# A later transposition, later weight sums and other buffer counts in a two-layer trunk kernel

## The chip, the cores and the metric

The kernel runs on one core of a Trainium2 chip. The metric is the device time in microseconds of one execution: 992.76 us is the median of 3 runs (991.8 to 993.68).

## The reference

The reference is a decoder trunk of two layers on 256 tokens of width 1024. Each layer is a half-step SwiGLU FFN, a token-mixing sublayer with one input projection and one output projection, and a second FFN, each followed by a layer norm:

```python
def swiglu(x, w_gate, w_up, w_down):
    return (jax.nn.silu(x @ w_gate) * (x @ w_up)) @ w_down

for l in range(DEPTH):
    x = layer_norm(ALPHA * x + 0.5 * swiglu(x, ffn1_gate[l], ffn1_up[l], ffn1_down[l]), ...)
    ...                                  # mixing: short conv, spatial gating, sparse attention
    x = layer_norm(ALPHA * x + mix, ...)
    x = layer_norm(ALPHA * x + 0.5 * swiglu(x, ffn2_gate[l], ffn2_up[l], ffn2_down[l]), ...)
```

All weights are float32, and the inner width of an FFN is 2816. The change touches the FFNs alone, and the pools from which all stages take their buffers.

## The kernel before

**Split weights.** Every product is made of three matmuls, of a rounded high part and a remainder of each operand (`mm3`, L246, and L258 to L260). A block of the weight stream (128x1024, 512 KB) is loaded into a `raw` buffer by SyncE; ScalarE casts it to a `hi` tile (L190), and VectorE subtracts to get the `lo` tile (L191). There are 5 `raw`, 12 `hi` and 12 `lo` buffers. A `hi` or `lo` buffer comes free when the last matmul that reads it has ended; `raw` when VectorE has read it. `ensure` (L167) writes the blocks down in the order of the stream, some seven blocks ahead of the product that needs them.

**Order.** The program is written in the order of the code. A planner with a cost model of its own then lays out each engine's queue before the run: it goes through simulated time and gives a free engine the earliest written instruction that is ready and for which a buffer is free (silu and product in the chunks of 256 count as written somewhat earlier, L544, L560). On the chip each queue runs in the order so fixed, and an instruction that waits holds up those behind it.

**FFN.** The inner width is cut into a chunk 0 of 512 columns and nine chunks of 256. In chunk 0 the products keep tokens on the partitions: gate of tile 0 (`pg`), up of tile 0 (`pu`), gate of tile 1, up of tile 1 (`tok`, L398), each 24 matmuls of 512 columns. Their PSUM banks alternate between two (`gu_bank`, L149), so that up of tile 1 is written to the bank of up of tile 0, and gate of tile 1 to that of gate of tile 0. ScalarE makes `sg` (silu, L421), VectorE `h = pu * sg` (L426, called `product`). `h` is transposed by TensorE (`trans`, L435, four transpositions of 128x128), copied to `hf` (L443) and split into `hTh` and `hTl` (L263). In the chunks of 256 the products have the inner width on the partitions (`chan`, L408, 48 matmuls of 256 columns) and need no transposition.

**Paired chunks.** In three of the four FFNs (all but the first of layer 0) the down products of chunks 0 to 5 are made with seven matmul triples M1 to M7 in place of eight (`paired`, L476). Their right operands come from two `raw` blocks of the stream (`pair_operands`, L196): M1 from a tile `b11` (one tile holds both its parts), M2 and M3 from the halves of the second block, M4 to M7 from sums of quarters of both. The sums are subtractions of 128x512 in place in `raw` (L202); the casts of the two summed blocks to four tiles stand in `rest` (L219), which is put off until at least two more blocks of the stream are loaded, counted whenever a block is split (L193). M5 and M7 read the first, M4 and M6 the second of these. The left operands of M1, M2, M4 are parts of `hT`; those of M3, M5, M6, M7 come from `left_sums` (L458), four small VectorE sums `S` and one split into `hTh` and `hTl`. While chunks are paired, gate and up of a chunk share one PSUM bank, so up waits until `sg` has been read from it. Between gate and up of chunk c stand M1, M2, M4, M5 of chunk c-1 (12 matmuls of 512 columns, in chunk 0 twice as many); behind up stand M6, M7, M3. M3 has a bank of its own, which a later chunk uses. `combine` (L487) adds the seven results to the residual.

Of the kernel before, what the change touches and what calls it, by code (L numbers as in the profile page):

```python
# [34 lines left out]
def _paired(l, f):  # L35

    return 0 if (l, f) == (0, 1) else 6
# [95 lines left out]
def _build(tc, A, out):  # L133
# [3 lines left out]
    with ExitStack() as es:  # L137
        pool = lambda name, bufs, **k: es.enter_context(tc.tile_pool(name=name, bufs=bufs, **k))
        cst = pool("cst", 1)
        rawp = pool("raw", 5)  # L140
        hip = pool("hi", 12)
        lop = pool("lo", 12)
        wk = pool("wk", 9)
        sm = pool("sm", 3)
        lnp = pool("lnp", 1)
# [3 lines left out]
        def gu_bank(shape, name):  # L149
            turns.append(1)  # L150
            return ps.tile(shape, F32, name=name, tag=f"gu{len(turns) % 2}", bufs=1)
# [9 lines left out]
        loaded = []  # L161
# [3 lines left out]
        put_off = []  # L165

        def ensure(i):  # L167
            while len(loaded) <= min(i, len(plan) - 1):
                key, k, n, split, o = plan[len(loaded)]
                src = A["ws"][o:o + 128 * n].rearrange("(p c) -> p c", p=128)  # L170
                if len(key) == 4 and key[2] == "d" and key[3] < _paired(*key[:2]):
                    raw = rawp.tile([128, n], F32, name="raw", tag="raw")
                    stream.append(SP.dma_start(raw, src))
                    if k % 2 == 0:
                        loaded.append(raw)
                    else:
                        loaded[-1], rest = pair_operands(loaded[-1], raw)
                        loaded.append(loaded[-1])
                        put_off.append((len(loaded), rest))
                    continue  # L180
                if not split:
                    raw = (hip, lop)[k % 2].tile([128, n], F32, name="w1", tag=("hi", "lo")[k % 2])
                    SP.dma_start(raw, src)
                    loaded.append((raw, None))
                    continue
                raw = rawp.tile([128, n], F32, name="raw", tag="raw")
                stream.append(SP.dma_start(raw, src))
                hi = hip.tile([128, n], F32R, name="hi", tag="hi")
                lo = lop.tile([128, n], F32R, name="lo", tag="lo")
                splits.append((ACT.copy(hi, raw),  # L190
                               DVE.tensor_tensor(lo, raw, hi.bitcast(F32), ALU.subtract)))  # L191
                loaded.append((hi, lo))
                while put_off and put_off[0][0] < len(loaded) - 1:  # L193
                    put_off.pop(0)[1]()

        def pair_operands(ra, rb):  # L196
# [39 lines left out]
        def kslices(key, n, ahead=None):  # L236

            res = []
            for hi, lo in blocks(key, ahead):
                m = hi.shape[1] // n  # L240
                res += [(hi[:, i * n:(i + 1) * n], lo[:, i * n:(i + 1) * n]) for i in range(m)]
            return res
# [3 lines left out]
        def mm3(o, a, b, start, stop):  # L246

            PE.matmul(o, lhsT=a[0], rhs=b[0], start=start, stop=False)  # L248
            PE.matmul(o, lhsT=a[0], rhs=b[1], start=False, stop=False)  # L249
            return PE.matmul(o, lhsT=a[1], rhs=b[0], start=False, stop=stop)  # L250
# [34 lines left out]
        def xT(t, k):  # L285
            c = slice(t * 128, t * 128 + 128)
            return xTh[:, k, c], xTl[:, k, c]
# [102 lines left out]
        def ffn(l, f, lni, last=False, mid=None):  # L390
            n = len(CHUNKS)
            paired_chunks = _paired(l, f)
# [5 lines left out]
            def tok(name, t, in_y=False, ahead=None):  # L398

                w = kslices((l, f, name, 0), 512, ahead)  # L400
                if in_y:
                    p = ps.tile([128, 512], F32, name="p" + name, tag="y", bufs=4)
                else:
                    p = gu_bank([128, 512], "p" + name)
                products[:] = [mm3(p, xT(t, k), w[k], k == 0, k == KC - 1) for k in range(KC)]
                return p
# [17 lines left out]
            def product(p, sg):  # L424
                h = wk.tile([128, 512], F32, name="h", tag="w")
                DVE.tensor_tensor(h, p.rearrange("p a b -> p (a b)") if len(p.shape) == 3 else p, sg, ALU.mult)  # L426
                return h
# [3 lines left out]
            def hpair():  # L431
                return (wk.tile([128, 512], F32R, name="hTh", tag="a"),
                        wk.tile([128, 512], F32R, name="hTl", tag="a"))

            def trans(h, t):  # L435
                tr = ps.tile([128, 512], F32, name="tr", tag="tr")
                for i in range(4):
                    c = slice(i * 128, i * 128 + 128)
                    PE.transpose(tr[:, c], h[:, c], ident)
                hT[0, t] = hpair()  # L440
                if paired_chunks:
                    hf[t] = wk.tile([128, 4, 128], F32, name="hf", tag="w")
                    ACT.copy(hf[t].rearrange("p a b -> p (a b)"), tr)  # L443
                    tr = hf[t].rearrange("p a b -> p (a b)")
                split_to(*hT[0, t], tr)
# [30 lines left out]
            def paired(c, ms):  # L476

                for m in ms:
                    if m not in M:
                        tag, bufs = {3: (held, 1), 6: ("tr", 2), 7: ("tr", 2)}.get(m, ("y", 4))  # L480
                        M[m] = ps.tile([128, 512], F32, name=f"M{m}", tag=tag, bufs=bufs)
                    for i in range(CHUNKS[c][1] // 256):
                        w = blocks((l, f, "d", c))[2 * i]
                        mm3(M[m], left_side(c, i, m), w[m], c == 0 and i == 0,
                            c == paired_chunks - 1 and i == CHUNKS[c][1] // 256 - 1)
# [36 lines left out]
            h = {}  # L522
            if l == 0 and f == 1:
                sg = [gated(tok("g", 0, True, ahead=0))]
                with ExitStack() as order:
                    for i in second_x(products):
                        order.enter_context(tc.issue_after(i.ins))
                    ensure(index[l, f, "g", 0][-1] + 3)
                sg.append(gated(tok("g", 1, True)))
                h = {t: product(tok("u", t), sg[t]) for t in range(2)}  # L530
                trans(h[0], 0)
            else:
                for t in range(2):
                    sg = gated(tok("g", t))
                    if t == 1:
                        trans(h[0], 0)
                    h[t] = product(tok("u", t), sg)

            if paired_chunks:
                turns.append(1)  # L540
                free, held = f"gu{len(turns) % 2}", f"gu{1 - len(turns) % 2}"
            for c in range(1, n):
                p = chan("g", c)
                with tc.high_priority(offset=60):  # L544
                    sg = gated(p)
                if c == 1:
                    trans(h[1], 1)
                if c <= paired_chunks:
                    if c == 1:
                        for i in range(2):  # L550
                            a = lambda t, b: hf[t][:, 2 * i + b, :]
                            left_sums(0, i, a(0, 0), a(0, 1), a(1, 0), a(1, 1))
                    paired(c - 1, (1, 2, 4, 5))
                elif not paired_chunks:
                    if c > 1 and c - 2 < n - late:
                        down([c - 2], 1)
                    if c - 1 < n - late:
                        down([c - 1], 0)
                pu = chan("u", c)
                with tc.high_priority(offset=60):  # L560
                    hc = product(pu, sg)
                if c <= paired_chunks:
                    paired(c - 1, (6, 7, 3))
                hT[c] = hpair()
                split_to(*hT[c], hc)
                if c < paired_chunks:
                    a = lambda t, b: hc[:, b * 256 + t * 128:b * 256 + t * 128 + 128]
                    left_sums(c, 0, a(0, 0), a(0, 1), a(1, 0), a(1, 1))
                if c == paired_chunks:
                    combine()  # L570
                if c == 2:
                    with tc.issue_after(stream[-1].ins):
                        gb = load_ln(l, lni)
                if c == 4 and mid:
                    with tc.issue_after(stream[-1].ins):
                        mid()
# [362 lines left out]
```

## Time and profile before

| | |
|---|---|
| median of 3 runs | 992.76 us (991.8 to 993.68) |
| the profiled execution | 994.34 us, of which the span from first to last instruction is 992.6 us |
| TensorE (PE) busy | 969.1 us, 98% of the span |
| TensorE weight load (PEld) | 875.8 us, 88% |
| VectorE (DVE) | 734.8 us, 74% |
| ScalarE (ACT) | 512.3 us, 52% |
| mean granted TensorE clock | 0.999 |
| weight blocks (512 KB), issue to landing | 4.6 us median |

Times in the rows are microseconds from the first instruction unless marked ns. In a timeline a row is: start, length, engine, line of the kernel, operation, what it writes and reads, shape, count, and in brackets how long the engine had been idle before it and what ended that. `x4` means four instructions merged in one row. PE overlaps matmuls, so a row's length is more than the step from one start to the next.

### The profile page before, as it was taken

The numbers are of one execution on the slowest core, as the hardware profiler recorded it, in microseconds if no ns is written. First come the engines' busy times: TensorE is split into PE (matmuls) and PEld (weight loads), VectorE is DVE, ScalarE is ACT, GpSimd is POOL, SyncE is SP. The second block draws the span as 40 slices with busy tenths as digits, with TensorE's granted clock in tenths as the row PEclk, the third lists the DMA queues.
The fourth block names the chain that finished last, engine by engine and source line by source line (L and its number), as shares of the span: only waits on it lengthen the run. The fifth ranks groups of instructions, "written<-read, shape, count | busy, mean of one in ns | idle before, by whom it ended". The sixth has DMA issues, their size and how long they took to land.

```text
span 992.6 us, 16879 instructions
## 1 busy us (share of the span) xinstructions
PE 969.1 (98%) x6765; PEld 875.8 (88%) x6765; DVE 734.8 (74%) x1094; ACT 512.3 (52%) x730; POOL 19.8 (2%) x42
## 2 busy tenths in 40 slices
PE   7999999999999999999999999999999999999996
PEld 5899999899878799999879899998988778989995
DVE  5755454586869978877598888848678797888844
ACT  6644444256556655555255556534475555556520
POOL 1000000010000000000000000000000000000000
PEclk9999999999999999999999999999999999999999
DMA  7977566284323557677245667764742245757611
GB/s 256 344 237 226 181 194 193 96 324 147 111 86 128 179 180 236 194 253 233 86 151 171 233 214 253 237 200 148 256 149 80 84 158 170 253 196 232 213 60 43
DMA packets 53069, 183.19 MB, mean 185 GB/s; under 512 B 6656, under 2 KB 7168, under 8 KB 52992
## 3 DMA queue, kind: packets, MB, share of 16 engines
q1 hardware_dynamic: 52992, 182.12, 55.0%
q8 instruction: 53, 0.87, 0.4%
q14 instruction: 24, 0.20, 0.1%
HBM read 181.05 MB, written 1.05 MB: 183 GB/s over the span
## 4 chain that ended last, share of the span: by engine, by line
PE 74%; DVE 11%; DMA 9%; issue 3%; ACT 3%; SPq 0%; DVEq 0%; ACTq 0%
DMA raw<-in_ws 8%; PE pu L258 6%; PE pu L260 6%; PE pu L259 6%; PE pg L258 5%; PE pg L260 5%; PE pg L259 5%; PE y L248 4%; PE y L250 4%; PE y L249 4%; DVE raw L202 3%; PE pc L258 3%; PE pc L260 3%; PE pc L259 3%; DVE lo L263 3%
## 5 line engine op out<-in xcount | busy, mean ns | idle before, releaser
L191 DVE TENSOR_TENSOR lo<-raw,hi 128x1024 fp32r<-128x1024 f32 (+3 forms) x284 | 336.6, 1200 | 115.2 <-ACT hi L190 113.5
L190 ACT CAST hi<-raw 128x1024 fp32r<-128x1024 f32 (+3 forms) x284 | 289.8, 1034 | 247.4 <-PE pu L259 64.7
L258 PE MATMUL pu<-xTh,hi 128*128 128x256 f32 x576 | 161.7, 281 | 3.4 <-ACT sg L421 3.4
L258 PE MATMUL pg<-xTh,hi 128*128 128x256 f32 x576 | 161.6, 281 | 0.5 <-DVE h L426 0.5
L260 PE MATMUL pu<-xTh,lo 128*128 128x256 f32 x576 | 160.9, 279 | 0.0
L260 PE MATMUL pg<-xTh,lo 128*128 128x256 f32 x576 | 160.8, 279 | 0.0
L259 PE MATMUL pu<-xTl,hi 128*128 128x256 f32 x576 | 160.8, 279 | 0.0
L259 PE MATMUL pg<-xTl,hi 128*128 128x256 f32 x576 | 160.8, 279 | 0.0
L258 PEld LDWEIGHTS pu<-xTh,hi 128*128 128x128 f32 x576 | 108.0, 188 | 7.1 <-ACT sg L421 5.9
L263 ACT CAST hi<-raw 128x1024 fp32r<-128x1024 f32 x63 | 66.2, 1052 | 90.5 <-DVE raw L202 46.5
L258 PEld LDWEIGHTS pg<-xTh,hi 128*128 128x128 f32 x576 | 108.1, 188 | 2.3 <-DVE h L426 1.2
L259 PEld LDWEIGHTS pu<-xTl,hi 128*128 128x128 f32 x576 | 107.9, 187 | 1.2
L260 PEld LDWEIGHTS pu<-xTh,lo 128*128 128x128 f32 x576 | 108.2, 188 | 0.2
L259 PEld LDWEIGHTS pg<-xTl,hi 128*128 128x128 f32 x576 | 107.9, 187 | 0.5
L260 PEld LDWEIGHTS pg<-xTh,lo 128*128 128x128 f32 x576 | 108.2, 188 | 0.0
L263 DVE TENSOR_TENSOR lo<-raw,hi 128x1024 fp32r<-128x1024 f32 x63 | 76.7, 1219 | 30.6 <-ACT hi L263 21.7
L258 PE MATMUL pc<-xTh,hi 128*128 128x256 f32 x256 | 73.0, 285 | 0.5 <-DVE kd L630 0.5
L248 PE MATMUL y<-hi,hTh 128*128 128x512 f32 x184 | 72.4, 394 | 0.0
L260 PE MATMUL pc<-xTh,lo 128*128 128x256 f32 x256 | 72.4, 283 | 0.0
L259 PE MATMUL pc<-xTl,hi 128*128 128x256 f32 x256 | 71.8, 281 | 0.0
L250 PE MATMUL y<-hi,hTl 128*128 128x512 f32 x184 | 71.8, 390 | 0.0
L249 PE MATMUL y<-lo,hTh 128*128 128x512 f32 x184 | 71.6, 389 | 0.0
(188 smaller groups left out, 1702.0 us busy)
## 6 DMA issues: line engine op xcount, KB each, us to landing
raw<-in_ws SPq DMA_DIRECT2D x312, 512.0 KB, 4.6
w<-in_ws SPq DMA_DIRECT2D x8, 512.0 KB, 6.2
lng<-in_ln SPq DMA_DIRECT2D x6, 512.0 KB, 6.8
lnb<-in_ln SPq DMA_DIRECT2D x6, 512.0 KB, 7.7
raw<-in_ws SPq DMA_DIRECT2D x8, 256.0 KB, 4.8
raw<-in_ws SPq DMA_DIRECT2D x4, 420.0 KB, 4.3
x<-in_x SPq DMA_DIRECT2D x4, 256.0 KB, 5.6
out<-x SPq DMA_DIRECT2D x4, 256.0 KB, 2.1
```

The lines of the kernel that those rows point to most:

```text
L190: splits.append((ACT.copy(hi, raw), DVE.tensor_tensor(lo, raw, hi.bitcast(F32), ALU.subtract)))
L191: DVE.tensor_tensor(lo, raw, hi.bitcast(F32), ALU.subtract)))
L202: sub = lambda o, i, j: DVE.tensor_tensor(o, i, j, ALU.subtract)
L248: PE.matmul(o, lhsT=a[0], rhs=b[0], start=start, stop=False)
L249: PE.matmul(o, lhsT=a[0], rhs=b[1], start=False, stop=False)
L250: return PE.matmul(o, lhsT=a[1], rhs=b[0], start=False, stop=stop)
L258: PE.matmul(p[:, b, :], lhsT=hi, rhs=xTh[:, k, :], start=k == 0, stop=False)
L259: PE.matmul(p[:, b, :], lhsT=hi, rhs=xTl[:, k, :], start=False, stop=False)
L260: PE.matmul(p[:, b, :], lhsT=lo, rhs=xTh[:, k, :], start=False, stop=k == KC - 1)
L263: return ACT.copy(hi, src), DVE.tensor_tensor(lo, src, hi.bitcast(F32), ALU.subtract)
```

## The change

It moves the transposition of `h` of tile 0 behind up of tile 1 in the FFNs with paired chunks; it asks for three more blocks, in place of two, before `rest` is written down (for the first pair of an FFN the count is passed at the same block either way, since the second pair counts too); it exchanges the places of M3 and M4; and it takes 7 `raw` buffers and 11 `hi` and 11 `lo`, so that the memory taken stays the same.

```diff
-        rawp = pool("raw", 5)
-        hip = pool("hi", 12)
-        lop = pool("lo", 12)
+        rawp = pool("raw", 7)
+        hip = pool("hi", 11)
+        lop = pool("lo", 11)
...
-                while put_off and put_off[0][0] < len(loaded) - 1:
+                while put_off and put_off[0][0] < len(loaded) - 2:
                     put_off.pop(0)[1]()
...
                 for t in range(2):
                     sg = gated(tok("g", t))
-                    if t == 1:
+                    if t == 1 and not paired_chunks:
                         trans(h[0], 0)
                     h[t] = product(tok("u", t), sg)
+                if paired_chunks:
+                    trans(h[0], 0)
...
-                    paired(c - 1, (1, 2, 4, 5))
+                    paired(c - 1, (1, 2, 3, 5))
...
-                    paired(c - 1, (6, 7, 3))
+                    paired(c - 1, (6, 7, 4))
```

All FFNs that take the branch with the moved `trans` have paired chunks.

## Rows read from the trace of the kernel before

**Rows 1.** The page: busy time, share of the span, instructions of each engine.

```profile
PE   969.1 (98%) x6765; PEld 875.8 (88%) x6765; DVE 734.8 (74%) x1094; ACT 512.3 (52%) x730; POOL 19.8 (2%) x42
```

**Rows 2.** Waits of PE: who waited for whom, us in total, times, longest.

```profile
PE tr L439 <- DVE h L426: 4.5, 3, 1.8
PE pu L258 <- ACT sg L421: 3.4, 6, 1.2
PE pg L258 <- DVE h L426: 0.5, 1, 0.5
```

**Rows 3.** Timeline of PE, second FFN of layer 0, end of gate of tile 1.

```profile
329.34 0.39 PE L249 MATMUL pg<-lo,xTh 128*128 128x512 f32 x1
329.57 0.40 PE L250 MATMUL pg<-hi,xTl 128*128 128x512 f32 x1
331.74 0.63 PE L439 MATMUL tr<-ident,h 128*128 128x128 f32 x4 [1.77 <-DVE h L426]
332.12 0.48 PE L248 MATMUL pu<-hi,xTh 128*128 128x512 f32 x1
```

**Rows 4.** Timeline of PE at the same place of the second FFN of layer 1.

```profile
818.65 0.63 PE L439 MATMUL tr<-ident,h 128*128 128x128 f32 x4 [1.50 <-DVE h L426]
```

**Rows 5.** Timeline of DVE before the first of these stalls.

```profile
324.49 1.28 DVE L202 TENSOR_TENSOR raw<-raw 128x512 f32<-128x512 f32 x2
325.69 1.22 DVE L191 TENSOR_TENSOR lo<-raw,hi 128x1024 fp32r<-128x1024 f32 x1
...
329.17 1.22 DVE L263 TENSOR_TENSOR lo<-raw,hi 128x1024 fp32r<-128x1024 f32 x1
...
330.91 0.68 DVE L426 TENSOR_TENSOR h<-pu,sg 128x512 f32<-128x512 f32 x1
```

**Rows 6.** Timeline of ACT in the same stretch: casts of weight blocks.

```profile
319.80 1.04 ACT L190 CAST hi<-raw 128x1024 fp32r<-128x1024 f32 x1
...
325.81 1.06 ACT L263 CAST hi<-raw 128x1024 fp32r<-128x1024 f32 x1 [4.00 <-DVE raw L202]
327.20 1.05 ACT L263 CAST hi<-raw 128x1024 fp32r<-128x1024 f32 x1 [0.34 <-PE pg L250]
```

**Rows 7.** Timeline of ACT before two silus in paired chunks.

```profile
383.13 1.05 ACT L263 CAST hi<-raw 128x1024 fp32r<-128x1024 f32 x1 [2.05 <-DVE raw L202]
384.09 0.58 ACT L421 ACTIVATE sg<-pg 128x512 f32<-128x512 f32 x1
...
432.25 1.05 ACT L190 CAST hi<-raw 128x1024 fp32r<-128x1024 f32 x1 [1.60 <-DMA raw<-in_ws]
```

**Rows 8.** Timeline of PE in paired chunks, six places.

```profile
384.73 0.38 PE L258 MATMUL pu<-xTh,hi 128*128 128x256 f32 x1 [0.52 <-ACT sg L421]
...
400.28 0.39 PE L248 MATMUL M<-hi,hTh 128*128 128x512 f32 x1
...
524.99 0.28 PE L258 MATMUL pg<-xTh,hi 128*128 128x256 f32 x1
...
853.61 0.39 PE L248 MATMUL M<-hi,hTh 128*128 128x512 f32 x1
...
869.76 0.39 PE L248 MATMUL M<-hi,hTh 128*128 128x512 f32 x1
...
872.00 0.38 PE L258 MATMUL pu<-xTh,hi 128*128 128x256 f32 x1 [0.72 <-ACT sg L421]
```

**Rows 9.** Timeline of DVE at three of these places.

```profile
518.16 1.23 DVE L191 TENSOR_TENSOR lo<-raw,hi 128x1024 fp32r<-128x1024 f32 x1 [0.80 <-ACT hi L190]
...
849.94 0.69 DVE L263 TENSOR_TENSOR hTl<-S,hTh 128x512 fp32r<-128x512 f32 x1
...
869.03 0.69 DVE L263 TENSOR_TENSOR hTl<-S,hTh 128x512 fp32r<-128x512 f32 x1
```

**Rows 10.** Waits of ACT for a freed buffer of gate weights.

```profile
ACT hi L190 <- PE pg L259: 45.4, 37, 2.9
```

**Rows 11.** Busy time of each engine in the first 40 us of one FFN.

```profile
312.00:352.00 40.00, 38.23 (x205) 32.10 (x204) 36.78 (x54) 23.27 (x29) 0.99 (x1) 1.00 0.53 175
```

## The prediction, made before the changed kernel was run

> **What bounds the kernel now.** I read the page first, then the waits of TensorE, then the timelines around each of them. The page shows PE busy for 969.1 of 992.6 us [rows 1]: matmuls follow one another, 0.23 us apart at 512 columns (329.57 − 329.34, [rows 3]). DVE is second with 74%. So the order of the work matters only where PE stands still, or where it would begin to. The waits of PE that lie in the FFNs are three [rows 2]: 4.5 us in 3 waits for `h` (the transposition of tile 0, once in each FFN with paired chunks), 3.4 us in 6 waits of `pu` for `sg`, and 0.5 us for a product. Together 8.4 us, 0.85% of the span; that is the most that these edits can win. No row of PE's waits names a split weight, so the weights are always early.
>
> **Part 1: `trans` of tile 0 behind up of tile 1.** Gate of tile 1 ends its starts at 329.57, the transposition starts at 331.74 after 1.77 us of idling, and up of tile 1 comes right behind it at 332.12 [rows 3]; in layer 1's second FFN the idle time is 1.50 us [rows 4], and the three are the 4.5 us [rows 2]. It looks as if PE waited for something that it could do later. But up of tile 1 goes to the PSUM bank of up of tile 0, and that bank is free only when `h` of tile 0 has been read from it. Moved to the front, `pu` waits for the same instruction at 330.91 to 331.59 [rows 5]. By itself this edit wins nothing and costs nothing: the four transpositions are as many as before, and behind up of tile 1 they find `h` ready for 5 us. What follows from them (copy, split, left sums) is late by about one product, 24 × 0.23 = 5.5 us, but M1 needs it only after gate of chunk 1, 48 matmuls later, and the left sums wait for tile 1 anyway.
>
> The Trainium skill (PSUM — Partial Sum Buffer, "PSUM bank collisions raise a hardware error") says that two engines must be kept apart by the bank, whatever addresses in it they touch. By that rule the stall outlives the moved transposition, and the sum would lack its first term; the rows agree as far as they go, since `pu` never starts before `h` ends.
>
> What decides is therefore when DVE does `h` of tile 0. Gate of tile 1 began at 329.57 − 23 × 0.23 = 324.3, so up of tile 0 had ended by 324.5; yet `h` starts at 330.91: DVE works without a break through weight sums (L202) and casts [rows 5], and over these 40 us it is busy for 36.78 [rows 11]. Its queue is laid out by the planner: whatever is written earlier and ready goes first. Three remainders of 1.22 us stand before `h`: of a gate block of chunk 1 (325.69) and of the first pair's two summed blocks (the second at 329.17). Why were they ready? Count the `hi` buffers when gate of tile 1 starts: four for gate, four for up, 1 for one `b11` (the other is in `lo`), 2 for the second blocks of the pairs: 11. The twelfth holds the gate block of chunk 1, cast at 319.80 [rows 6], before any gate block of chunk 0 is free. The next casts, 325.81 and 327.20, take buffers that gate of tile 1 gives back, the second explicitly (`PE pg`).
>
> **Part 2: 11 `hi` and `lo`.** With 11 buffers that block can't be cast at 319.80. It waits for the first gate block to come free, at about 325.7, and its remainder is ready at 326.8 rather than in time for 325.69. The summed blocks follow one buffer later each, 1.4 us (6 × 0.23) apart. From 324.5 on the planner then finds DVE between the links of the chain of weight sums with no cast ready, and `h`, ready since 324.5, is next. I expect it at 325 to 328, before gate of tile 1 ends at 330. Then PE doesn't stop: −4.5 us in three places. The other end: the planner keeps the order. The third gate block is free at 324.3 + 3 × 1.4 = 328.5, cast by 329.5, its remainder done by 330.7, and with one sum of 0.68 us behind it `h` starts at 331.4, 0.5 us later than now: +1.5 in three places. I take −4.5, because the row at 319.80 shows that it was the twelfth buffer which let the cast in.
>
> The price of a buffer less elsewhere is lead. A paired chunk takes 7.5 buffers of each kind (2 gate, 2 up, 3.5 for the pair) in about 16 us, so one is 2.1 us. The least lead of a split weight over its first matmul in the FFNs after the first is the second gate block of chunk 1 in the FFN of layer 1: remainder done at 518.16 + 1.23 = 519.39 [rows 9], first used at 524.99 [rows 8], 5.6 us. 2.1 leaves 3.5 us: nothing. If the lead were used up by two buffers more, each late buffer would show as up to 2.1 us at PE. M3 ahead of M5 also gives the second block's tiles back in the first group, some 9 us earlier, which pays for part of the twelfth buffer.
>
> The Trainium skill (Perfetto Trace Analysis, "Optimization Strategy") reads a gap that repeats as a sign that there are too few buffers for the next tile. By that rule 11 would lengthen the three stalls: the +1.5 end, 6 us above my sum. Here the rows speak against it: the gap ends with `h`, not with a cast, and what stands in the way is work let in early.
>
> **Part 3: weight sums cast a block later, 7 `raw`.** `sg` at 384.09 stands behind a cast that waited 2.05 us for a weight sum of DVE [rows 7], and `pu` idles 0.52 us for it [rows 8]. Of the six waits for `sg` four are of this kind (2.65 us, the first 0.52 and the last 0.72 [rows 8]); in the other two (0.70 us) the cast ahead of `sg` waited for a DMA, as the one at 432.25 did for 1.60 us. With `rest` a block later an up block, whose data need no sum, is in that place, and with 7 `raw` it has been loaded sooner (a pair holds its two `raw` buffers a block longer, so of two added one is left). Bounds: all 3.9 us of `sg` and `pg` gone; or the up block waits there for a buffer, 45.4/37 = 1.23 us in the mean [rows 10], at four places: 4.9 − 2.65 = +2.3. I take half of the 2.65: −1.3. The sums' own users lose nothing: the block cast at 383.13 is read by M5 at 400.28 [rows 7, 8]. More DMAs in flight (two blocks) cost nothing, since PE waits for none behind the first.
>
> **Part 4: M4 behind M3.** M3 starts where M4 did and so needs the left sums 3 × 0.23 = 0.7 us sooner than M5 does now. In the 15 chunks 1 to 5 of three FFNs the margin from the remainder of `S` to that place runs from 0.05 us (869.71 to 869.76) to 2.98 us (850.63 to 853.61) [rows 8, 9]; the remainder is read only by the third matmul, 0.46 us on. As it stands no M3 waits. If `S` comes one cast (1.22 us) later, four chunks wait, 1.4 us in all. I take +0.3. In chunk 0 both M3 and M5 wait for `S`, and up of chunk 1, 5.7 us, is there to be put between. M4's later end holds a pair of `hT` buffers longer; 8 of the 9 are then taken, none is missing.
>
> **Sum.** −4.5 − 1.3 + 0.3 = −5.5 us: a span of 987.1 and, with the 1.7 us around it, 988.8 for the profiled execution (994.3). That execution is 1.6 us over the median, so the median comes to 992.8 − 5.5 = **987.3 us**.
>
> **Rivals.** *The stall stays.* `h` remains where it is in DVE's queue and `pu` waits in place of the transposition. Only parts 3 and 4 count: 992.8 − 1.0 = 991.8. For it: DVE is 92% busy there, and the sums' chain alone is written before `h`. Against: the casts that filled the gaps lack a buffer.
>
> *M3 waits for the left sums.* The three FFNs keep DVE so busy that `S` ends two casts (2.44 us) later than now, since up blocks and sums have traded places. Then 11 of the 15 chunks wait, 9.05 us by their margins, and even with the 4.5 us won the time is 992.8 + 9.05 − 4.5 = 997.3. It decides from a delay of about 1.9 us. Behind a waiting M3 stand M5 and up of the next chunk, so PE stops. For it: the margin of 0.05 us. Against: in the chunks shown the summed blocks' casts come behind `S`, so a later cast does not push it.
>
> *Everything goes.* All 8.4 us: 984.4. The edits do aim at each wait, but a queue fixed by a model rarely meets all.
>
> **Chances.** Forecast 0.55, stall stays 0.22, M3 waits 0.15, everything 0.08. A measurement of this kernel tells 0.2% (2 us) from no change: below 990.8 is faster, above 994.7 slower. Faster: 0.52 of the forecast, 0.02 of the second (its part 3 can win more), 0.08: 0.62. Same: 0.03 + 0.14 = 0.17. Slower: 0.06 (the second with +1.5 and +2.3) + 0.15 = 0.21. The likeliest case alone runs from 984.7 to 990.9 (part 3 at its ends). The range is 984.0 to 995.0: all but the third rival.
>
> **What would show it.** Right: `h` of tile 0 starts before 329 in DVE's timeline of the first paired FFN, `pu` follows `pg` without idle time, and PE's waits name neither `h` for the transposition nor for `pu`. The first cast of a chunk 1 block falls behind the first matmuls of gate of tile 1. Part 3: an L190 cast ahead of `sg`, and less than 2 us of `pu` waits. Wrong: a wait `PE pu <- DVE h` of 4 to 6 us (first rival); waits of M for `hTh` or `hTl` in most chunks (second); any wait of PE for `lo` (the lead was misjudged).

## The result: 1.5% slower, and the profile after

The changed kernel takes 1008.15 us (4 runs, 1006.3 to 1008.31) beside 993.22 us for the kernel before on the same chip: a ratio of 1.0148 (95% interval 1.0131 to 1.0166). Forecast was 987.3 us with a range to 995.0; it went the other way, by nearly three times the size.

The page of the changed kernel, engines' busy time, against [rows 1]: PE works 8.5 us longer for the same matmuls, and the span is 14.0 us longer (1006.6 us).

```profile
PE 977.6 (97%) x6761; PEld 882.2 (88%) x6765; DVE 733.6 (73%) x1094; ACT 513.8 (51%) x730; POOL 24.9 (2%) x42
```

What PE waited for in the changed kernel (us in total, times, longest), against [rows 2]:

```profile
PE pu L248 <- DVE h L426: 6.4, 3, 2.5
PE pg L258 <- ACT sg L421: 4.9, 3, 1.7
...
PE M L248 <- ACT hTh L263: 0.6, 3, 0.3
```

The six waits of `pu` for `sg` in the chunks are gone. In place of the 4.5 us ahead of the transposition there are 11.3 us, in two stalls per FFN. The timeline of PE at the first of them, against [rows 3]:

```profile
331.07 0.40 PE L250 MATMUL pg<-hi,xTl 128*128 128x512 f32 x1
333.10 0.38 PE L258 MATMUL pg<-xTh,hi 128*128 128x256 f32 x1 [1.63 <-ACT sg L421]
336.00 0.80 PE L248 MATMUL pu<-hi,xTh 128*128 128x512 f32 x1 [2.52 <-DVE h L426]
336.59 0.63 PE L249 MATMUL pu<-lo,xTh 128*128 128x512 f32 x1
337.02 0.63 PE L250 MATMUL pu<-hi,xTl 128*128 128x512 f32 x1
```

A single matmul of gate of chunk 1 has come between gate and up of tile 1. It waits until `sg` of tile 1 has been read from its bank, then up of tile 1 waits for `h`. Behind that the matmuls of up start 0.43 us apart (337.02 − 336.59), not 0.23. The windows of the changed kernel show why (after the engines' busy times: granted TensorE clock, DMA share, GB/s):

```profile
331.00:336.00 5.00, 0.85 (x3) 0.21 (x3) 4.95 (x6) 1.70 (x3) 0.00 (x0) 0.94 0.68 201
336.00:341.00 5.00, 5.00 (x12) 3.94 (x13) 0.95 (x1) 1.05 (x1) 0.00 (x0) 0.50 0.66 219
```

PE was busy for 0.85 us of 5, and then the granted clock is 0.50, the lower level (1.2 GHz), for the next 5 us. Up of tile 1 takes 8.5 us from its first start to what PE does next, 5.7 us before (337.8 − 332.1).

DVE before this stall, against [rows 5]; the casts of ACT in the same stretch, against [rows 6]:

```profile
327.10 2.50 DVE L202 TENSOR_TENSOR raw<-raw 128x512 f32<-128x512 f32 x4
329.50 1.23 DVE L191 TENSOR_TENSOR lo<-raw,hi 128x1024 fp32r<-128x1024 f32 x1
330.64 0.70 DVE L202 TENSOR_TENSOR raw<-raw 128x512 f32<-128x512 f32 x1
331.24 1.23 DVE L263 TENSOR_TENSOR lo<-raw,hi 128x1024 fp32r<-128x1024 f32 x1
332.37 0.70 DVE L202 TENSOR_TENSOR raw<-raw 128x512 f32<-128x512 f32 x1
332.98 1.23 DVE L263 TENSOR_TENSOR lo<-raw,hi 128x1024 fp32r<-128x1024 f32 x1
334.11 1.23 DVE L191 TENSOR_TENSOR lo<-raw,hi 128x1024 fp32r<-128x1024 f32 x1
335.25 0.70 DVE L426 TENSOR_TENSOR h<-pu,sg 128x512 f32<-128x512 f32 x1
```

```profile
327.30 1.05 ACT L190 CAST hi<-raw 128x1024 fp32r<-128x1024 f32 x1 [2.68 <-PE pg L250]
328.70 1.05 ACT L263 CAST hi<-raw 128x1024 fp32r<-128x1024 f32 x1 [0.35 <-PE pg L250]
330.10 1.06 ACT L263 CAST hi<-raw 128x1024 fp32r<-128x1024 f32 x1 [0.35 <-PE pg L250]
331.50 1.05 ACT L190 CAST hi<-raw 128x1024 fp32r<-128x1024 f32 x1 [0.35 <-PE pg L250]
332.45 0.59 ACT L421 ACTIVATE sg<-pg 128x512 f32<-128x512 f32 x1
```

The casts come as forecast, each when a gate block is given back, 1.4 us apart. But `h` has not passed them: it stands behind all of them, and behind one more (334.11). Likewise `sg` stands behind the fourth cast of ACT.

**Where the 14.0 us come from,** by the starts of the same products in both traces:

| stretch | change, us |
|---|---|
| gate of tile 1 to gate of chunk 2, three paired FFNs | +5.9, +3.9, +5.6 |
| output product of the two mixing stages to gate of tile 1 behind it | +1.7, +1.8 |
| gate of chunk 2 to the end of the three FFNs | −1.6, −2.6, −1.6 |
| the rest | +0.9 |

Of the +15.4 us in the first row 6.8 us are the 24 matmuls of up of tile 1 at the lower clock (2.8, 1.6, 2.5); most of the rest is the 6.8 us more of idling (11.3 − 4.5).

### The profile page after: what moved, and what is told of

Same layout as the page of the kernel before. It is cut to its first block, busy times and chain, and to the rows that moved or that the text cites. A ratio compares the mean times of both kernels' runs of the same rounds, so it can differ in the third digit from the quotient of the medians.

```text
span 1006.6 us, 16881 instructions
## 1 busy us (share of the span) xinstructions
PE 977.6 (97%) x6761; PEld 882.2 (88%) x6765; DVE 733.6 (73%) x1094; ACT 513.8 (51%) x730; POOL 24.9 (2%) x42
## 4 chain that ended last, share of the span: by engine, by line
PE 86%; DVE 9%; issue 2%; ACT 2%; DMA 0%; SPq 0%; DVEq 0%; ACTq 0%
PE pg L258 7%; PE pg L260 7%; PE pg L259 7%; PE pu L258 6%; PE pu L260 6%; PE pu L259 6%; PE y L248 4%; PE y L250 4%; PE y L249 4%; PE M L248 3%; PE M L250 3%; PE M L249 3%; PE pc L260 3%; PE pc L258 3%; PE pc L259 3%; DVE lo L191 2%
```

## The experiments

Theory A put the harm on the buffer counts, theory B on the moved transposition. Medians and ratios to the kernel before, which ran beside them:

| kernel | us | ratio (95%) |
|---|---|---|
| trans_only | 993.05 | 0.9996 (0.9982 to 1.0009) |
| bufs_only | 1007.57 | 1.0140 (1.0120 to 1.0161) |
| all_but_bufs | 996.9 | 1.0021 (1.0002 to 1.0040) |
| after_h60 | 988.0 | 0.9945 (0.9925 to 0.9966) |
| split_only | 1007.46 | 1.0138 (1.0122 to 1.0154) |
| raw6_only | 1001.3 | 1.0067 (1.0046 to 1.0089) |
| before_h60 | 992.43 | 0.9987 (0.9973 to 1.0001) |
| r6_h60 | 983.79 | 0.9898 (0.9880 to 0.9916) |
| after_fill16 | 1001.47 | 1.0069 (1.0050 to 1.0088) |
| m_only | 995.38 | 1.0004 (0.9991 to 1.0018) |
| late_only | 992.7 | 0.9986 (0.9970 to 1.0002) |
| a12r6_h60 | 984.53 | 0.9898 (0.9875 to 0.9920) |
| after_h60_at200 | 990.05 | 0.9969 (0.9958 to 0.9981) |

**trans_only**

```diff
-                    if t == 1:
+                    if t == 1 and not paired_chunks:
                         trans(h[0], 0)
                     h[t] = product(tok("u", t), sg)
+                if paired_chunks:
+                    trans(h[0], 0)
```

> Only the transposition of tile 0 is moved behind up of tile 1; everything else as before. Theory A (the buffer counts did the harm: with 11 split-weight buffers and 7 raw buffers, h of tile 0 falls behind more casts in VectorE's queue, and the order of the end of mixing changes): no change, 991 to 995 us, and up of tile 1 waits for h for the same 4.5 us that the transposition waited. Theory B (the moved transposition did the harm, since gate of chunk 1 now stands in the gap): slower by 6 to 14 us, 999 to 1007.

No change, as theory A says. PE's waits in this kernel, and the row of its first stall:

```profile
PE pu L248 <- DVE h L426: 4.3, 3, 1.5
```

```profile
328.66 0.50 PE L248 MATMUL pu<-hi,xTh 128*128 128x512 f32 x1 [1.54 <-DVE h L426]
```

`pu` stands where the transposition stood, for the same instruction. The bank holds it, as the prediction and the rule of the Trainium skill beside it said (PSUM — Partial Sum Buffer, "PSUM bank collisions raise a hardware error").

**bufs_only** and **all_but_bufs**

```diff
-        rawp = pool("raw", 5)
-        hip = pool("hi", 12)
-        lop = pool("lo", 12)
+        rawp = pool("raw", 7)
+        hip = pool("hi", 11)
+        lop = pool("lo", 11)
```

> Only the buffer counts are changed (7 raw, 11 hi, 11 lo). Theory A: the stalls at the start of the three paired FFNs with the clock's fall behind them (+15 us in the changed kernel) and the end of mixing (+5 us) are all there, while the wins in the paired chunks (-6 us) need the later casts: 1008 to 1014 us. Theory B: no change, 990 to 996.

> The three other edits with the old counts (5 raw, 12 hi, 12 lo). Theory A: no start stall beyond the 4.5 us of before, no change at the end of mixing, and part of the wins in the paired chunks: 987 to 992 us. Theory B: 999 to 1007. A third possibility: with 5 raw buffers the later casts starve the stream, since a pair holds its raw buffers a block longer: waits of PE for lo, slower than 995.

The buffer counts alone make 1.40% of the 1.48%, and without them the rest is near the time before. It did not win as I had forecast for theory A (987 to 992 us). I expected the wins in the chunks to need the later casts; they do not: in bufs_only `pu` never waits for `sg`, and the stretch from gate of chunk 2 to the end (the third row of the table above) wins 1.4 to 2.5 us in each FFN here too. The other three edits together change the place of the waits: the `sg` waits go, and `pg` waits for `h` in the chunks, as the waits of PE in all_but_bufs show; M waits 2.6 us for `hTh` there too.

```profile
PE pg L258 <- DVE h L426: 6.7, 4, 2.1
```

**after_h60** (the whole change, with `h` early)

```diff
                     if t == 1 and not paired_chunks:
                         trans(h[0], 0)
-                    h[t] = product(tok("u", t), sg)
+                    pu = tok("u", t)
+                    with tc.high_priority(offset=60):
+                        h[t] = product(pu, sg)
```

> The whole change, and the product h of chunk 0 in paired FFNs counts for the planner as written 60 instructions earlier, so that it passes the casts in VectorE's queue. Theory A: h of tile 0 starts within 2 us of the end of up of tile 0, PE does not stop between gate and up of tile 1, the clock stays at its higher level there, and about 15 us come back: 990 to 996 us (the +5 us at the end of mixing and the -6 us in the chunks stay). If the clock fell for another reason than these stalls, only the stalls themselves (some 9 us) come back: 998 to 1001. Theory B: 1004 or more.

20 us come back, more than the 15 that I had charged to the stalls, since the 4.5 us of before go too. DVE and PE of this kernel at the place of the stall:

```profile
325.94 0.69 DVE L426 TENSOR_TENSOR h<-pu,sg 128x512 f32<-128x512 f32 x1
```

```profile
331.05 0.39 PE L250 MATMUL pg<-hi,xTl 128*128 128x512 f32 x1
331.28 0.39 PE L248 MATMUL pu<-hi,xTh 128*128 128x512 f32 x1
```

The edit touches nothing but the priority of `h`: it runs 9.3 us earlier, and there is no stall. The window 336 to 341 has a granted clock of 1.00 again.

**split_only** and **raw6_only** (11 `hi` and `lo` with 5 `raw`; 6 `raw` with 12 and 12)

```diff
-        hip = pool("hi", 12)
-        lop = pool("lo", 12)
+        hip = pool("hi", 11)
+        lop = pool("lo", 11)
```

```diff
-        rawp = pool("raw", 5)
+        rawp = pool("raw", 6)
```

> Before with 11 hi and 11 lo and still 5 raw buffers. Theory C (the raw buffers make the start stalls, since more blocks of the stream are loaded and cast ahead of h; the missing split buffer changes only the end of mixing): slower by the two ends of mixing alone, some 5 us: 996 to 1000 us, start stalls 3 to 6 us in all, clock at its higher level there. Theory D (the missing split buffer makes the start stalls, each cast coming one freed buffer later ahead of h): 1008 us or more.

> Before with 6 raw buffers and still 12 hi and lo (7 and 12 do not fit into the memory). Theory C: the stalls at the start of the paired FFNs are as in the changed kernel, with one matmul of gate of chunk 1 ahead of up of tile 1 and the clock's fall: +15 us there, -5 us of the waits for sg in the chunks, the end of mixing as before: 1000 to 1006 us. Theory D: only the chunk waits go: 987 to 990 us.

Neither theory was right alone: each count makes start stalls, by a way of its own. PE's waits in split_only, then in raw6_only:

```profile
PE tr L439 <- DVE h L426: 9.4, 3, 3.5
...
PE pu L258 <- ACT sg L421: 4.1, 3, 1.5
```

```profile
PE tr L439 <- DVE h L426: 5.1, 3, 2.0
PE pg L258 <- ACT sg L421: 5.0, 3, 1.7
```

With a split buffer fewer, `h` stands behind the same three casts as before, but these come later; DVE of split_only (first and last of the three, and `h`):

```profile
329.85 1.22 DVE L191 TENSOR_TENSOR lo<-raw,hi 128x1024 fp32r<-128x1024 f32 x1
...
333.32 1.22 DVE L263 TENSOR_TENSOR lo<-raw,hi 128x1024 fp32r<-128x1024 f32 x1
334.46 0.69 DVE L426 TENSOR_TENSOR h<-pu,sg 128x512 f32<-128x512 f32 x1
```

With a `raw` buffer more, two more casts have their data in time and go ahead of `h`; DVE of raw6_only (the two, and `h`):

```profile
330.38 1.22 DVE L191 TENSOR_TENSOR lo<-raw,hi 128x1024 fp32r<-128x1024 f32 x1
331.51 1.22 DVE L263 TENSOR_TENSOR lo<-raw,hi 128x1024 fp32r<-128x1024 f32 x1
332.65 0.69 DVE L426 TENSOR_TENSOR h<-pu,sg 128x512 f32<-128x512 f32 x1
```

And the matmul of gate of chunk 1 is in the gap only with more `raw`. Its first block is split before the gap either way; what differs in the traces is `sg` of tile 1, which frees its bank. In raw6_only `sg` comes ahead of `h` (330.47 and 332.65), in split_only behind it (335.58 and 334.46), since the cast ahead of it has waited for a DMA. ACT of raw6_only, then of split_only:

```profile
330.47 0.59 ACT L421 ACTIVATE sg<-pg 128x512 f32<-128x512 f32 x1
```

```profile
334.62 1.05 ACT L190 CAST hi<-raw 128x1024 fp32r<-128x1024 f32 x1 [3.14 <-DMA raw<-in_ws]
335.58 0.59 ACT L421 ACTIVATE sg<-pg 128x512 f32<-128x512 f32 x1
```

The `raw` count also wins the `sg` waits in the chunks (none in raw6_only, 4.1 us in split_only). The longer end of mixing (second row of the table of stretches) is in every kernel with 11, at least 1.7 us each time, and in none with 12, within 0.1 us of before.

**before_h60** and **r6_h60** (the earlier `h` in the kernel before, with 5 and with 6 `raw`)

```diff
-        rawp = pool("raw", 5)
+        rawp = pool("raw", 6)            # r6_h60 alone
...
-                    h[t] = product(tok("u", t), sg)
+                    pu = tok("u", t)
+                    with tc.high_priority(offset=60):
+                        h[t] = product(pu, sg)
```

> Before, with h of chunk 0 counted as written 60 instructions earlier for the planner. If h's place in VectorE's queue is all that stops PE at the start of these FFNs, the 4.5 us go and the waits for sg in the chunks stay: 987 to 990 us. If PE then finds another wait there (left sums, a late split weight): 991 to 994.

> Before with 6 raw buffers, 12 hi and lo, and h 60 instructions earlier. If the raw buffers win the chunk waits and do harm only through h's place: -4.5 and -4.9 us, 982 to 986 us, faster than the kernel before and than the changed kernel with h earlier (988.0). If the chunk waits need the seventh buffer or the later casts: 987 to 990 us.

With 5 `raw` most of the 4.5 us are given back elsewhere. PE's waits in before_h60:

```profile
PE pu L258 <- ACT sg L421: 4.5, 6, 1.4
...
PE M L248 <- ACT hTh L263: 2.5, 3, 0.8
```

With 6 it is 9.8 us faster than the kernel before (993.61 us beside it), 1.0%, the best version of the study. PE's waits in its FFNs add up to little; the largest kind:

```profile
PE pg L258 <- DVE h L426: 0.4, 1, 0.4
```

**after_fill16** (the whole change, with PE kept busy)

```diff
+                    if t == 1:
+                        fill = ps.tile([128, 512], F32, name="fill", tag="tr")
+                        for k in range(16):
+                            PE.matmul(fill, lhsT=xTh[:, k % KC, 0:128], rhs=xTh[:, 0:2, :], start=True, stop=True)
                     if t == 1 and not paired_chunks:
```

> The whole change, and between gate and up of tile 1 of the paired FFNs 16 matmuls of 512 columns (some 3.7 us) into a spare PSUM bank whose result nobody reads: PE has work while it would wait for sg and h. Theory E (the clock falls because PE stood idle there): up of tile 1 starts within 0.5 us of where it does in the changed kernel, its 24 matmuls stay 0.23 us apart, and 5 to 7 us come back in spite of 48 added matmuls: 1001 to 1004 us. Theory F (the clock falls for another reason, such as the change of matmul shapes): no win, 1007 to 1010 us.

48 useless matmuls make the changed kernel 6.7 us faster (1008.15 − 1001.47; by the ratios, since the chips differ, 0.8%). Up of tile 1 starts as late as without them (10.3 us behind the first matmul of gate of tile 1 in both), but PE has not stood still for long, and the clock stays at the higher level. PE at the first stall, and the window that follows:

```profile
335.80 0.28 PE L259 MATMUL pg<-xTl,hi 128*128 128x256 f32 x1
336.73 0.50 PE L248 MATMUL pu<-hi,xTh 128*128 128x512 f32 x1 [0.65 <-DVE h L426]
```

```profile
336.00:341.00 5.00, 4.35 (x19) 3.49 (x19) 1.98 (x4) 2.10 (x2) 0.00 (x0) 1.00 0.82 257
```

**m_only** and **late_only**

```diff
-                    paired(c - 1, (1, 2, 4, 5))
+                    paired(c - 1, (1, 2, 3, 5))
...
-                    paired(c - 1, (6, 7, 3))
+                    paired(c - 1, (6, 7, 4))
```

```diff
-                while put_off and put_off[0][0] < len(loaded) - 1:
+                while put_off and put_off[0][0] < len(loaded) - 2:
```

> Before with M3 and M4 exchanged, nothing else. If the left sums are in time as their margins in the trace of before say: 992 to 995 us and less than 1.5 us of waits of M. If the exchange makes the new waits of the kernel with all edits but the buffers (M for hTh 2.6 us, pg for h 6.7 us): 995 to 999.

> Before with the casts of the weight sums a block later, nothing else. If these casts were what held up sg: the waits of pu for sg go, 988 to 991 us. If with 5 raw buffers they starve the stream or fall ahead of the product h instead: the waits change place (pg for h), 993 to 998 us.

Neither changes the time by more than can be told. M waits for `hTh` for 0.4 us in m_only, so the left sums are in time. What the exchange does is to turn the waits for `sg` into waits of `pg` for `h`; PE's waits in m_only:

```profile
PE pg L258 <- DVE h L426: 4.6, 3, 2.4
```

In late_only `pu` still waits for `sg`, 2.7 us in place of 3.4.

**a12r6_h60** (all edits, 6 `raw`, 12 and 12, `h` early)

```diff
-        rawp = pool("raw", 7)
-        hip = pool("hi", 11)
-        lop = pool("lo", 11)
+        rawp = pool("raw", 6)
+        hip = pool("hi", 12)
+        lop = pool("lo", 12)
```

> All edits of the change, but with 6 raw, 12 hi and 12 lo buffers, and h counted as written 60 instructions earlier. Beside the kernel that has 6 raw buffers and the earlier h alone (983.8): if the moved transposition, the later casts and the exchange are worth nothing once the waits are gone, 983 to 985 us; if they cost as they do with 5 raw buffers, 986 to 989; if they win, below 982.

As fast as r6_h60 within the intervals: the moved transposition, the later casts and the exchange are worth nothing once the waits are gone. Beside after_h60 (988.0) it shows what the twelfth split buffer and 6 in place of 7 `raw` are worth together when `h` is early: 3.5 us by the medians, 0.5% by the ratios, since the chips differ. The traces show some 1.7 us of it at each of the two ends of mixing.

**after_h60_at200** (after_h60 with the attention steps early)

```diff
-                    attend(t, slots, sc.pop(i))
+                    with tc.high_priority(offset=200):
+                        attend(t, slots, sc.pop(i))
```

> The whole change with h counted as written 60 instructions earlier, and the instructions of each attention step (maximum, exponentials, scaling, transposition) as written 200 earlier, so that they pass the casts of later weights in VectorE's and ScalarE's queues. If with 11 split buffers the end of mixing is longer because casts that come late stand ahead of the last heads' scaling: the 0.9 us stalls of PE at the end of both mixing stages go and about 5 us come back, 982 to 985 us (the same kernel without it: 988.0). If the end of mixing is longer for another reason (the output product's buffers): 987 to 990.

Not settled: the two late stalls at the end of mixing in after_h60 (0.7 us for `P`, 0.6 us for `xTh`, once each in both stages) go, but others come earlier in the same stage, and the time is 2 us longer than without. PE's waits in this kernel:

```profile
PE o L862 <- ACT PT L843: 1.4, 2, 0.7
...
PE trp L841 <- DVE P L837: 1.0, 2, 0.5
PE scm L815 <- ACT P L830: 1.0, 2, 0.5
```

That the end of mixing depends on the twelfth split buffer is shown; by what way is open.

## Why the prediction was wrong

**Part 1 held.** The moved transposition is worth nothing (0.9996), and `pu` waits in its place.

**Part 2 is the step that failed.** Its first half was right: the block that the twelfth buffer let in is cast only when a gate block comes free, and the others follow 1.4 us apart. The second half, "on the planner then finds DVE between the links of the chain of weight sums with no cast ready, and `h` … is next", was wrong. DVE's four sums stand back to back (327.10 to 329.60) and then the casts, each with a sum behind it; `h` found no gap; that the planner's model had something written earlier ready each time is inferred from this order, its own times are not on record. So the later casts did not let `h` pass, they pushed it. I set the other end at +1.5 us, by when the buffers come free. But DVE's own work sets it: in split_only three remainders and two sums follow the four sums without a break, from 329.85 to `h` at 334.46. split_only has 9.4 us of these waits, 4.9 more than before, and the whole kernel 11.3. The rule of the Trainium skill that I set aside (Perfetto Trace Analysis, "Optimization Strategy": a gap that repeats can mean too few buffers for the next tile) had the direction right: one split buffer fewer doubled that gap. It was no full account of it: one `raw` buffer more lengthened it as well.

**Three prices were missing.** First, 7 `raw` was costed at nothing, "since PE waits for none": what more loaded blocks do to the queues of ACT and DVE was not asked. Second, a stall was charged its own length; here its shadow at the lower clock cost as much again (6.8 us; after_fill16 gives back 6.7). Third, the lead of 5.6 us that a split weight has was read for the FFNs alone, and 11 buffers were not costed at the end of mixing, which lost 1.7 and 1.8 us.

**Part 3 won more, for another reason.** I took −1.3 us; the chunks gained 5.8 us. But the later casts are not the cause (late_only): the `raw` buffers are, and with them ACT's waits for the stream go. ACT's waits of the kernel before, then of the changed one, then of raw6_only:

```profile
ACT hi L190 <- DMA raw<-in_ws: 49.3, 51, 2.9
...
ACT hi L263 <- DVE raw L202: 46.5, 21, 5.1
```

```profile
ACT hi L263 <- DVE raw L202: 14.2, 8, 1.9
...
ACT hi L190 <- DMA raw<-in_ws: 6.3, 8, 2.1
```

```profile
ACT hi L263 <- DVE raw L202: 47.6, 21, 5.1
...
ACT hi L190 <- DMA raw<-in_ws: 14.9, 26, 2.1
```

The waits of casts for weight sums, by which I had explained four of the six `sg` waits, are as long in raw6_only as before (47.6 and 46.5 us), and yet `pu` waits for no `sg`. Nor were the 8.4 us of idle time the most that could be won. At the seven waits in the chunks of the kernel before (3.8 us) the starts of PE's matmuls lie 4.9 us further apart than without a wait, as at the first, which ends at 384.73 [rows 8]: 0.91 us in place of 0.23, for 0.52 us idle. The remaining 0.9 of the 5.8 us I can't place. PE just before it:

```profile
383.82 0.39 PE L250 MATMUL M<-hi,hTl 128*128 128x512 f32 x1
```

**Part 4 held for M.** M waits 0.6 us in the changed kernel and 0.4 in m_only, +0.3 forecast. What it lacked is that the exchange turns the waits for `sg` into waits for `h` when there are 5 `raw`. The slower rival (M3 waits for the left sums) had the sign by the wrong mechanism; the rival "the stall stays" was nearest, and it lacked that the stall could grow.

## What to carry to other kernels

Where a planner lays out in-order queues, a buffer is also an admission ticket: one more or one fewer changes which work stands ahead of the instruction that the bound engine waits for. Before costing a count, find that instruction, list what is written ahead of it, and ask of each when it will be ready; then put it ahead by priority and change the counts afterwards. Here, with `h` put ahead, 6 `raw` and 12 split buffers won 1.0% (r6_h60), where that count alone had lost 0.7%, and 7 and 11 with the other edits won 0.5% (after_h60), where the counts alone had lost 1.4%.

## What the hardware showed that I had not expected

Stalls of 1.2 to 1.8 us alone at this place (kernel before, trans_only: 1.3 to 1.5), and one of 2.4 us in split_only, left the granted clock at 1.00. Two stalls with a single matmul between them (1.63 and 2.52 us, or 1.68 and 1.40 us, in the changed kernel), or one of 3.5 us (split_only: 0.66 in the 5 us from 336), were followed by the lower level. Up of tile 1 then took 8.5, 7.2 and 8.1 us in the changed kernel in place of 5.7. Work whose result nobody reads, put into the gap, kept the higher level.
